# Memory tokens of a two-layer encoder: divided by their root mean square and transposed once, scaled per layer by column; head roots spread by full transposes

## The chip, the cores and the metric

One core of a Trainium2 chip runs the whole program in one launch. The metric is the time of one execution in device microseconds (us). The kernel before ran three times: 1570.52, 1573.77 and 1574.49 us, median 1573.77. One more execution was profiled; it took 1572.0 us, of which 1570.2 us lie between its first and its last recorded instruction (the span).

Engines in the rows: PE is the matrix engine (PEld its weight loads), DVE the vector engine, ACT the scalar engine, POOL the GpSimd, SP the engine that issues nearly all DMAs (SPq is its queue).

## The reference

The reference is an encoder trunk of two layers on x (512 tokens, width 1024), with 256 memory tokens of the same width. What the change touches:

```python
for l in range(2):
    h = rmsnorm(x, g_mix_pre[l])
    ...                                   # h @ w_in[l], split into three head groups
    o_a = diff_attention(...)             # 4 heads, 64 values each
    o_a = rmsnorm(o_a, diff_head_g[l]) * (1.0 - lam_init)     # a norm per head of 64 values
    ...                                   # latent attention o_b, windowed attention o_c
    x = x + rmsnorm(concat([o_a, o_b, o_c]) @ w_out[l], g_mix_post[l])
    xo = cross_attention(rmsnorm(x, g_x_pre[l]), rmsnorm(mem, g_x_mem[l]), w_xq[l], w_xkv[l], w_xo[l])
    x = x + rmsnorm(xo, g_x_post[l])
    ...                                   # SwiGLU feed-forward, added to x in the same way

def rmsnorm(x, g):
    return x * rsqrt(mean(x * x, axis=-1) + 1e-6) * g
```

The memory `mem` is the same in both layers; only its gains `g_x_mem[l]` differ.

## The kernel before

All products take their factors as a high part (type fp32r) and a low part (what the rounding left), and three matmuls stand for one product (`mm3`, lines 149 to 153). A tensor therefore has to be *split*: ACT casts to the high part (L104), DVE subtracts it (L105). Weights come through a ring of two staging tiles `st` (`stage`, L113) and are split into tiles `wh` and `wl`.

A layer begins with `mix_phase`. Attention is cut into units (score, softmax, transposes, values); a loop over t starts one unit per step and runs the later stages of the earlier ones, and beside it draws steps from a generator `fill()`, which holds the products that attention doesn't wait for. How many steps it draws per t follows from the planned PE time of what it has drawn (`FILL_PLAN`, and `FILL_STEP` for each step). Units 0 to 15 are the differential heads (`diff_units`), then come the windowed and the latent ones. The fill is, in this order: the input products of the second pair of differential heads (`in_diff(w, hT, 1, q3b)`), of the windowed keys and values and of half of their queries; then by the string `FILL_ORDER` the steps "q" (other queries), "u" (latent up-projection), "m" (`mem_norm`) and "k" (`make_xK`, keys of the cross-attention); then values and output projection. The scheduler that assigns tiles and order keeps each engine's queue in one fixed order; an engine waits at the head of its queue.

PSUM has two tiles of each of the tags mm, sc, at and av. The tag "at" (name `ps_at`) is where every transpose lands: a transpose waits until one of the two tiles has been read out.

`mem_norm` (L1074 to L1090), in each layer: it loads the gains as a row broadcast over 128 partitions into the slot H3 (L251), loads each half row of the memory into a tile of the tag "o" (L1083), squares it on ACT into what later holds the high part `memTh` (L209) with the sums `rmemss`, forms the root `rmem` on POOL (L213, L214), multiplies by root and gains on DVE (L230), transposes eight blocks of 128x128 on PE (L184), and splits them on ACT and DVE into `memTh` and `memTl`; this for two groups of 128 tokens.

The norm of a differential head, once for each pair of heads (`means`, `rows_`, `norm`): POOL gives `drs`, 8 roots per token (L692); `rows_` turns them into two rows by four thin transposes (L697) and a copy (L698); `norm` spreads the rows over 64 partitions each by a matmul with two ones-rows `halves_r` (L702) and multiplies on DVE (L703).

## Time and profile before

| what | before |
|---|---|
| median of three runs | 1573.77 us |
| the profiled execution | 1572.0 us, span 1570.2 us |
| PE busy | 1545.4 us (98%), 8260 matmul records |
| DVE, ACT, POOL busy | 981.2, 800.4, 96.0 us |
| granted PE clock, mean | 0.995 |
| layer 0: mixing with its fill | about 60 to 300 us |
| layer 1: the same | about 835 to 1080 us |
| DMA | 167.97 MB |

A page of the profile gives the busy time of each engine over the span; a window gives the same for a stretch. Matmuls are pipelined: one of 128 columns is listed with 0.27 us, and the next starts sooner than that. A number in square brackets in a timeline row is how long that engine had been idle before the row, and what ended the idleness. PEclk is the granted clock of PE as a share of 2.4 GHz.

### The profile page before, as it was taken

What the parts mean: (1) busy time and instruction counts of PE and PEld (TensorE: products, weight loads), DVE (VectorE), ACT (ScalarE), POOL (GpSimd) and SP (SyncE); (2) the same over time, 40 slices, a digit from 0 to 9 for tenths busy, and PEclk for the clock granted to TensorE, in tenths of its full rate; (3) what the DMA queues carried; (4) which work ended last, traced back from release to release, by engine and by line L of the source; (5) the groups of instructions that cost most, each with busy time, mean ns of one, the idle gap of its engine ahead of it and who ended that gap; (6) DMA issues with size and microseconds to landing.
All of it is one profiled execution on the core that took longest, in us unless ns stands there. A gap on an engine that the chain in (4) does not pass through costs nothing.

```text
span 1570.2 us, 22003 instructions
## 1 busy us (share of the span) xinstructions
PE 1545.4 (98%) x8260; PEld 1314.0 (84%) x8260; DVE 981.2 (62%) x1933; ACT 800.4 (51%) x1743; POOL 96.0 (6%) x199
## 2 busy tenths in 40 slices
PE   9998999999999999999999999999999999999998
PEld 7887987899888888888888878778888888888886
DVE  7898886764653444455567988857646444444544
ACT  5578888554543222222356788975544532222221
POOL 3100000200200000000130000002002000000000
PEclk9999999999999999999999999999999999999999
DMA  5632651241243232332335234522403423233221
GB/s 164 171 83 88 214 167 46 63 161 54 81 156 112 81 108 81 106 109 81 102 116 145 56 136 163 168 58 90 148 30 104 136 81 107 81 109 106 83 79 54
DMA packets 130195, 167.97 MB, mean 107 GB/s; under 512 B 21796, under 2 KB 100774, under 8 KB 129320
## 3 DMA queue, kind: packets, MB, share of 16 engines
q1 hardware_dynamic: 130080, 166.56, 33.3%
q8 instruction: 65, 1.06, 0.3%
q14 instruction: 42, 0.34, 0.1%
q10 hardware_dynamic: 8, 0.01, 0.0%
HBM read 150.16 MB, written 10.09 MB: 102 GB/s over the span
## 4 chain that ended last, share of the span: by engine, by line
PE 44%; DVE 2%; ACT 2%; POOL 1%; issue 1%; POOLq 0%; DVEq 0%; ACTq 0%
PE ps_mm L153 7%; PE ps_mm L151 7%; PE ps_mm L152 7%; PE ps_av L152 3%; PE ps_av L151 3%; PE ps_av L153 3%; PE ps_sc L151 3%; PE ps_sc L153 3%; PE ps_sc L152 3%; PE ps_at L433 2%; PE ps_av L606 1%; PE ps_sc L818 1%; PE ps_av L607 1%; PE ps_sc L655 1%; ACT hxh L209 0%
## 5 line engine op out<-in xcount | busy, mean ns | idle before, releaser
L105 DVE TENSOR_TENSOR wl<-st,wh 128x512 fp32r<-128x512 f32 (+1 forms) x406 | 273.4, 686 | 249.6 <-ACT wh L104 249.0
L104 ACT CAST wh<-st 128x512 fp32r<-128x512 f32 (+1 forms) x406 | 243.7, 617 | 308.3 <-PE ps_mm L152 126.7
L153 PE MATMUL ps_mm<-hfh,wl 128*128 128x512 f32 (+1 forms) x384 | 142.8, 372 | 2.1 <-DVE wl L105 2.1
L151 PE MATMUL ps_av<-hfh,wh 128*128 128x512 f32 (+1 forms) x384 | 142.9, 372 | 0.0
L152 PE MATMUL ps_mm<-hfl,wh 128*128 128x512 f32 (+1 forms) x384 | 142.6, 371 | 0.0
L151 PE MATMUL ps_mm<-hfh,wh 128*128 128x512 f32 (+1 forms) x384 | 142.6, 371 | 0.0
L153 PE MATMUL ps_av<-hfh,wl 128*128 128x512 f32 (+1 forms) x384 | 142.6, 371 | 0.0
L152 PE MATMUL ps_av<-hfl,wh 128*128 128x512 f32 (+1 forms) x384 | 142.6, 371 | 0.0
L151 PE MATMUL ps_sc<-dwh,f 128*128 128x512 f32 (+1 forms) x322 | 125.1, 389 | 0.5 <-DVE faccSq L1276 0.5
L152 PE MATMUL ps_sc<-dwl,f 128*128 128x512 f32 (+1 forms) x322 | 124.9, 388 | 0.0
L153 PE MATMUL ps_sc<-dwh,f 128*128 128x512 f32 (+1 forms) x322 | 124.9, 388 | 0.0
L104 ACT CAST dwh<-st 128x1024 fp32r<-128x1024 f32 x40 | 40.1, 1050 | 157.0 <-PE ps_sc L153 153.3
L105 DVE TENSOR_TENSOR pl<-ps_at,ph 128x512 fp32r<-128x512 f32 (+1 forms) x128 | 82.6, 654 | 23.9 <-ACT ph L104 22.8
L153 PEld LDWEIGHTS ps_mm<-hfh,wl 128*128 128x128 f32 x384 | 72.3, 188 | 15.1 <-DVE wl L105 2.5
L213 POOL TENSOR_SCALAR rpost<-rpostss 128x1 f32<-128x1 f32 x23 | 11.6, 503 | 1167.8 <-ACT hTh L209 699.2
L151 PEld LDWEIGHTS ps_mm<-hfh,wh 128*128 128x128 f32 x384 | 72.4, 189 | 12.5
L152 PEld LDWEIGHTS ps_av<-hfl,wh 128*128 128x128 f32 x384 | 72.4, 188 | 12.5
L153 PEld LDWEIGHTS ps_av<-hfh,wl 128*128 128x128 f32 x384 | 72.3, 188 | 12.5
L151 PEld LDWEIGHTS ps_av<-hfh,wh 128*128 128x128 f32 x384 | 72.2, 188 | 12.4
L152 PEld LDWEIGHTS ps_mm<-hfl,wh 128*128 128x128 f32 x384 | 72.3, 188 | 12.3
L104 ACT CAST ph<-ps_at 128x512 fp32r<-128x512 f32 (+1 forms) x128 | 70.4, 561 | 23.8 <-PE ps_at L433 22.8
L433 PE MATMUL ps_at<-ident,e 128*128 128x128 f32 x480 | 77.0, 275 | 3.7 <-DVE memTl L105 2.1
(384 smaller groups left out, 3865.3 us busy)
## 6 DMA issues: line engine op xcount, KB each, us to landing
st<-in_w_ffn_in SPq DMA_DIRECT2D x44, 1024.0 KB, 4.9
st<-in_w_ffn_out SPq DMA_DIRECT2D x22, 1024.0 KB, 4.8
st<-in_w_xkv SPq DMA_DIRECT2D x16, 1024.0 KB, 5.4
st<-in_w_in SPq DMA_DIRECT2D x16, 512.0 KB, 4.8
st<-in_w_out SPq DMA_DIRECT2D x16, 512.0 KB, 5.0
st<-in_w_xq SPq DMA_DIRECT2D x8, 1024.0 KB, 5.5
st<-in_w_xo SPq DMA_DIRECT2D x8, 1024.0 KB, 5.0
q<-stg SPq DMA_DIRECT2D x48, 128.0 KB, 2.3
```

What stands on the lines that cost most here:

```text
L104: cast = nc.scalar.copy(hi, src)
L105: nc.vector.tensor_tensor(out=lo, in0=src, in1=hi.bitcast(F32), op=ALU.subtract)
L151: nc.tensor.matmul(ps, lhsT=lh, rhs=rh, start=first, stop=False)
L152: nc.tensor.matmul(ps, lhsT=lh, rhs=rl, start=False, stop=False)
L153: nc.tensor.matmul(ps, lhsT=ll, rhs=rh, start=False, stop=last)
L213: nc.gpsimd.tensor_scalar(out=r, in0=ms[:, 0:1], scalar1=ms[:, 1:2], scalar2=EPS, op0=ALU.add, op1=ALU.add)
L433: nc.tensor.transpose(pt[:, c * P:(c + 1) * P], e[:, k * P:(k + 1) * P], ident)
L606: nc.tensor.matmul(av, lhsT=v, rhs=hi, start=k == u["k0"], stop=False)
L607: nc.tensor.matmul(av, lhsT=v, rhs=lo, start=False, stop=k == u["k1"] - 1)
L655: nc.tensor.matmul(ps, lhsT=t[:, m, 0, i * P:(i + 1) * P], rhs=t[:, m, 1, :], start=True, stop=True)
L818: nc.tensor.matmul(ps, lhsT=mla["qT"][:, h, i * P:(i + 1) * P], rhs=mla["kT"][:, h, :], start=True, stop=True)
```

## The change

It makes three edits. `mem_prep`, new, runs once, as the first four steps of layer 0's fill: it loads the memory, takes the squares (ACT, into the PSUM tile that will hold the transposes), forms the roots (POOL), multiplies by them (ACT), transposes (PE), copies back to the "o" tile (ACT) and stores the result in DRAM as `mem_dram`, laid out with the model's columns on the partitions. In this layout a gain is one number per partition: `gmem` holds the gains of both layers, loaded once. `mem_norm` of each layer then loads `mem_dram` through a staging tile (8 KB per partition) and splits it in eight blocks of 256 tokens, with the gain as the scale of both instructions. The third edit is in the head norm: `spread_` copies each root 64 times along the free dimension on ACT, and four full 128x128 transposes put it on the partitions; the thin transposes, the matmul with `halves_r` and the set-up of `halves_r` go.

```diff
--- before.py
+++ after.py
@@ -277,7 +277,6 @@
     neghalf = cp.tile([P, 8], F32, tag="neghalf", name="neghalf")
     nc.gpsimd.memset(neghalf, -0.5)
     halves_c = cp.tile([P, 2], F32, tag="halves", name="halves")
-    halves_r = cp.tile([2, P], F32, tag="halvesr", name="halvesr")
     nc.gpsimd.memset(halves_c, 0.0)
     for b in range(2):
         nc.gpsimd.memset(halves_c[64 * b:64 * (b + 1), b:b + 1], 1.0)
@@ -297,6 +296,8 @@
     dist_dram = dp.tile([P, NT, S], F32, tag="distd", name="dist_dram")
     dist0 = ap.tile([P, NT, S], F32, tag="dist", name="dist")
     swd_dram = dp.tile([P, 1280], F32, tag="swdd", name="swd_dram")
+    mem_dram = dp.tile([P, KC, MEM], F32, tag="memd", name="mem_dram")
+    gmem = cp.tile([P, DEPTH * KC], F32, tag="gmem", name="gmem")
     cos1 = cp.tile([P, NT, 16], F32, tag="cos1", name="cos1")
     sin2 = mp.tile([P, NT, 32], F32, tag="sin2", name="sin2")
 
@@ -314,9 +315,6 @@
                           diff_lambda.rearrange("l a d -> (l a d)").unsqueeze(0).to_broadcast([P, DEPTH * 128]))
 
     def setup():
-        ph = psum("at")
-        nc.tensor.transpose(ph[0:2, 0:P], halves_c, ident)
-        nc.vector.tensor_copy(out=halves_r, in_=ph[0:2, 0:P])
         nc.vector.tensor_scalar(out=nsinks, in0=sinks, scalar1=-1.0, scalar2=None, op0=ALU.mult)
         lq = tmp("ph", (P, DEPTH * 2, 32))
         lpv = lp.rearrange("p l a b d -> p (l a) b d")
@@ -691,22 +689,21 @@
                                                op0=ALU.mult, op1=ALU.add)
                 nc.gpsimd.tensor_tensor(out=r, in0=r, in1=neghalf, op=ALU.pow)
 
-            def rows_(ch):
-                pt = psum("at")
-                for i in range(NT):
-                    nc.tensor.transpose(pt[0:2, i * P:(i + 1) * P], ch["r"][:, 2 * i:2 * i + 2], ident)
-                nc.scalar.copy(ch["sq"][0:2], pt[0:2])
+            def spread_(ch):
+                nc.scalar.copy(ch["sq"].rearrange("p (n d) -> p n d", d=64),
+                               ch["r"].unsqueeze(2).to_broadcast([P, 8, 64]))
 
             def norm(ch):
                 pr = psum("at")
-                nc.tensor.matmul(pr, lhsT=halves_r, rhs=ch["sq"][0:2], start=True, stop=True)
+                for i in range(NT):
+                    nc.tensor.transpose(pr[:, i * P:(i + 1) * P], ch["sq"][:, i * P:(i + 1) * P], ident)
                 nc.vector.scalar_tensor_tensor(out=ch["o"], in0=ch["o"], scalar=headg, in1=pr,
                                                op0=ALU.mult, op1=ALU.mult)
 
             return chunk_units(
                 score, soft, [[((hh, i), (hh, i + 1), 0, NT) for i in (0, 2)] for hh in range(2)],
                 lambda hh, k: aV[:, k, c, 2 * hh:2 * hh + 2, :].rearrange("p b d -> p (b d)"),
-                [sums_sq, means, nop, rows_, norm, chunk_out(lambda: mdst(c))])
+                [sums_sq, means, nop, spread_, norm, chunk_out(lambda: mdst(c))])
 
         def swa_units(cp_, ip, mdst):
 
@@ -885,7 +882,7 @@
             state["xq"] = [(t[:, 0, k, :], t[:, 1, k, :]) for k in range(KC)], st
 
         def fill():
-            for k, _ in enumerate(seq(in_diff(w, hT, 1, q3b), in_swa_kv(), in_swa_q(0))):
+            for k, _ in enumerate(seq(*([] if l else [mem_prep()]), in_diff(w, hT, 1, q3b), in_swa_kv(), in_swa_q(0))):
                 if k == 0:
                     head.settle()
                 yield
@@ -1071,22 +1068,45 @@
                 as_tile(st_["ps"][i], st_["C"], aT, i * P, 512, (2, 3), first=False)
                 done(i, accs[i], st_["ps"][i])
 
+    def mem_prep():
+
+        with nc.allow_non_contiguous_dma(reason="gains by column, once"):
+            nc.sync.dma_start(gmem, g_x_mem.rearrange("l (k p) -> p (l k)", p=P))
+        for t in range(2):
+            hs = []
+            ms = small(2, "rmemss")
+            for j in range(2):
+                m = tmp("o")
+                nc.sync.dma_start(m, mem[0, t * P:(t + 1) * P, 512 * j:512 * (j + 1)])
+                pt = psum("at")
+                nc.scalar.activation(pt, m, AF.Square, scale=1.0 / 32.0, accum_out=ms[:, j:j + 1])
+                hs.append((m, pt))
+            r = small(1, "rmem")
+            nc.gpsimd.tensor_scalar(out=r, in0=ms[:, 0:1], scalar1=ms[:, 1:2], scalar2=EPS, op0=ALU.add, op1=ALU.add)
+            nc.gpsimd.tensor_tensor(out=r, in0=r, in1=neghalf[:, :1], op=ALU.pow)
+            yield
+            for j, (m, pt) in enumerate(hs):
+                nc.scalar.activation(m, m, AF.Copy, scale=r)
+                for c in range(4):
+                    nc.tensor.transpose(pt[:, c * P:(c + 1) * P], m[:, c * P:(c + 1) * P], ident)
+                nc.scalar.copy(m, pt)
+                nc.sync.dma_start(mem_dram[:, 4 * j:4 * j + 4, t * P:(t + 1) * P], m.rearrange("p (c t) -> p c t", t=P))
+            yield
+
     def mem_norm(l):
         memT = Split8(("H2", "dist"), MEM, "memT")
 
         def gen():
-            g, = gains("H3", g_x_mem[l])
-            for t in range(2):
-                hs = []
-                for j in range(2):
-                    m = tmp("o")
-                    nc.sync.dma_start(m, mem[0, t * P:(t + 1) * P, 512 * j:512 * (j + 1)])
-                    hs.append(m)
-                parts = norm_to_T(hs, g, memT, t * P, "rmem", hs)
-                yield
-                for f in parts:
-                    f()
-                yield
+            st = stage((), KC, MEM)
+            nc.sync.dma_start(st, mem_dram)
+            for k in range(KC):
+                g = gmem[:, KC * l + k:KC * l + k + 1]
+                hi = memT.h(k)
+                nc.scalar.activation(hi, st[:, k, :], AF.Copy, scale=g)
+                nc.vector.scalar_tensor_tensor(out=memT.l(k), in0=st[:, k, :], scalar=g, in1=hi.bitcast(F32),
+                                               op0=ALU.mult, op1=ALU.subtract)
+                if k % 2:
+                    yield
         return memT, gen()
 
     def make_xK(l, memT):
```

How the instructions move, on two engines and one queue. First PE in layer 0, in the key half of the input product of the second differential pair (products L151 to L153 into `ps_mm`; L655, in the changed kernel L653, are scores; L433 are the transposes of the attention weights `e`). Before:

```order
L153 MATMUL ps_mm<-hTh_146,wl 128x512
L151 MATMUL ps_mm<-hTh_146,wh 128x512
L152 MATMUL ps_mm<-hTl_147,wh 128x512
L153 MATMUL ps_mm<-hTh_146,wl 128x512
L433 MATMUL ps_at<-ident,e 128x128 x4
L655 MATMUL ps_sc<-q_00_561 128x512 x2
L433 MATMUL ps_at<-ident,e 128x128 x4
```

And in the changed kernel (L1091 are the transposes of the memory, L941 one of a latent tile):

```order
L151 MATMUL ps_mm<-hTh_147,wh 128x512
L1091 MATMUL ps_at<-ident,o 128x128 x4
L152 MATMUL ps_mm<-hTl_148,wh 128x512
L1091 MATMUL ps_at<-ident,o 128x128 x4
L153 MATMUL ps_mm<-hTh_147,wl 128x512
L151 MATMUL ps_mm<-hTh_147,wh 128x512
L152 MATMUL ps_mm<-hTl_148,wh 128x512
L941 MATMUL ps_at<-ident,m 128x128
```

The first eight memory transposes stand sixteen products into this half; the first transposes of `e` come only after the second eight, one input product later, where the queue reads:

```order
L153 MATMUL ps_mm<-hTh_147,wl 128x512
L1091 MATMUL ps_at<-ident,o 128x128 x4
L152 MATMUL ps_mm<-hTl_146,wh 128x512
L1091 MATMUL ps_at<-ident,o 128x128 x4
L153 MATMUL ps_mm<-hTh_145,wl 128x512
L151 MATMUL ps_mm<-hTh_145,wh 128x512
L431 MATMUL ps_at<-ident,e 128x128 x8
```

Next the SP queue of layer 0 about that place. Before (L372 stores a table that POOL has built, L495 to L497 bring the second differential pair's queries and keys into place, L113 loads weights):

```order
L351 DMA dist_dram<-dist 128x2048
L113 DMA st<-in_w_in 128x8x256
L372 DMA swd_dram<-swd 128x1280
L113 DMA st<-in_w_in 128x8x64 x3
L495 DMA q_10_1040<-stg 32x2x512
L496 DMA q_10_1040<-stg 32x2x512
L497 DMA q_10_1040<-stg 32x1024
```

In the changed kernel:

```order
L349 DMA dist_dram<-dist 128x2048
L1080 DMA o<-in_mem 128x512 x2
L370 DMA swd_dram<-swd 128x1280
L113 DMA st<-in_w_in 128x8x256
L113 DMA st<-in_w_in 128x8x64
L1093 DMA mem_dram<-o 128x4x128 x2
L493 DMA q_10_1091<-stg 32x2x512
L1080 DMA o<-in_mem 128x512 x2
L494 DMA q_10_1091<-stg 32x2x512
```

The second two loads of the memory stand behind the first of the `q` transfers, and the weights of the windowed keys behind the store of the table.

Last PE in layer 1, where the memory's transposes of this layer stood. Before:

```order
L607 MATMUL ps_av<-pl,aV 128x256
L184 MATMUL ps_at<-ident,o 128x128 x8
L433 MATMUL ps_at<-ident,e 128x128 x4
L606 MATMUL ps_av<-ph,KScV 128x256
L800 MATMUL ps_at<-ident,m 96x128 x8
```

In the changed kernel:

```order
L605 MATMUL ps_av<-pl,aV 128x256
L431 MATMUL ps_at<-ident,e 128x128 x4
L797 MATMUL ps_at<-ident,m 96x128 x8
L151 MATMUL ps_mm<-wh,latT 128x384
L152 MATMUL ps_mm<-wl,latT 128x384
```

The eight transposes are gone from between the values of one unit (L607) and the transposes of the next (L433), and so are the eight that followed later in this layer.

## Rows read from the trace of the kernel before

**Rows 1.** The page's first part: busy time, share of the span, instructions.
```profile
PE 1545.4 (98%) x8260; PEld 1314.0 (84%) x8260; DVE 981.2 (62%) x1933; ACT 800.4 (51%) x1743; POOL 96.0 (6%) x199
```
**Rows 2.** Windows of layer 0: stretch, length, busy by engine, PEclk, DMA share, GB/s.
```profile
60.00:90.00 30.00, 30.00 (x150) 24.75 (x149) 27.00 (x72) 23.23 (x54) 4.34 (x12) 1.00 0.47 110
90.00:125.00 35.00, 34.88 (x188) 29.11 (x187) 33.43 (x83) 27.49 (x61) 1.65 (x1) 1.00 0.24 65
132.00:142.00 10.00, 6.02 (x39) 4.69 (x38) 7.80 (x22) 8.88 (x21) 0.00 (x0) 1.00 0.46 151
142.00:145.60 3.60, 3.60 (x18) 3.32 (x17) 3.11 (x12) 3.14 (x11) 0.86 (x2) 0.53 0.00 0
```
**Rows 3.** Windows of layer 1.
```profile
900.00:912.00 12.00, 11.98 (x72) 9.81 (x71) 11.05 (x31) 11.44 (x30) 1.80 (x3) 1.00 0.65 218
912.00:917.00 5.00, 2.73 (x19) 1.87 (x18) 4.68 (x11) 4.95 (x12) 0.00 (x0) 1.00 0.32 107
917.00:920.50 3.50, 3.50 (x17) 3.41 (x16) 2.94 (x11) 3.19 (x10) 0.86 (x2) 0.51 0.00 0
```
**Rows 4.** Timeline of PE, layer 0: start, us, line, operation, [idle before, who ended it].
```profile
137.71 1.35 PE L184 MATMUL ps_at<-ident,o 128*128 128x128 f32 x8 [0.59 <-DVE sr L742]
140.21 0.66 PE L433 MATMUL ps_at<-ident,e 128*128 128x128 f32 x4 [1.15 <-DVE memTl L105]
141.59 0.38 PE L606 MATMUL ps_av<-ph,KScV 128*128 128x256 f32 x1 [0.73 <-ACT ph L104]
```
**Rows 5.** Timeline of PE, layer 1, the same place.
```profile
913.07 1.35 PE L184 MATMUL ps_at<-ident,o 128*128 128x128 f32 x8 [0.53 <-DVE sr L742]
915.34 0.66 PE L433 MATMUL ps_at<-ident,e 128*128 128x128 f32 x4 [0.92 <-DVE memTl L105]
```
**Rows 6.** Timeline of ACT, layer 0: a weight cast that waits for its load.
```profile
133.04 0.62 ACT L104 CAST wh<-st 128x512 fp32r<-128x512 f32 x1 [1.62 <-DMA st<-in_w_xkv]
```
**Rows 7.** Timeline of PE, layer 0: the head norm's thin transposes and its matmul.
```profile
125.80 0.60 PE L697 MATMUL ps_at<-ident,drs 128*2 128x128 f32 x4
...
129.32 1.12 PE L702 MATMUL ps_at<-c,halvesr 2*128 2x512 f32 x2
```
**Rows 8.** Groups by line and shape: busy us, mean ns, idle before.
```profile
L209 ACT ACTIVATE memTh<-o 128x512 fp32r<-128x512 f32 x8 | 5.0, 627 | 0.0
L209 ACT ACTIVATION_READ_ACCUMULATOR memTh<-o 128x1 f32 x8 | 1.5, 191 | 0.0
L104 ACT CAST ph<-ps_at 128x512 fp32r<-128x512 f32 x112 | 64.9, 587 | 23.7 <-PE ps_at L433 22.8
L587 ACT ACTIVATE e<-e,mr 128x512 f32<-128x512 f32 x32 | 21.8, 734 | 0.1
L587 ACT ACTIVATE e<-e,sr 128x256 f32<-128x256 f32 x16 | 8.2, 513 | 1.7 <-DVE sr L742 1.7
L230 DVE SCALAR_TENSOR_TENSOR o<-o,rmem,gains 128x512 f32<-128x512 f32 x8 | 5.9, 743 | 1.0 <-POOL rmem L214 1.0
L105 DVE TENSOR_TENSOR memTl<-ps_at,memTh 128x512 fp32r<-128x512 f32 x8 | 5.5, 686 | 1.7 <-ACT memTh L104 1.7
```
**Rows 9.** One tile, `rmem`, on POOL: count, ns min/median/max, first and last start.
```profile
L213 POOL TENSOR_SCALAR rmem<-rmemss x4: 299/299/301, 127.4 to 918.2; 128x1 f32<-128x1 f32 x4
L214 POOL TENSOR_TENSOR rmem<-rmem,neghalf x4: 557/560/569, 127.7 to 918.6; 128x1 f32<-128x1 f32 x4
```
**Rows 10.** Timeline of ACT, layer 0, early: an exponential, the first casts of `ph`.
```profile
66.96 0.72 ACT L669 ACTIVATE e<-e,dnm 128x512 f32<-128x512 f32 x1 [0.23 <-DVE dnm L659]
...
73.42 1.07 ACT L104 CAST ph<-ps_at 128x512 fp32r<-128x512 f32 x2
```
**Rows 11.** Timeline of PE, layer 0, early: the first transposes of attention weights.
```profile
72.36 0.60 PE L433 MATMUL ps_at<-ident,e 128*128 128x128 f32 x4
```
**Rows 12.** Timeline of SP's queue: the first transfer of `q`.
```profile
73.54 0.62 SPq L495 DMA_DIRECT2D q<-stg  x1
```
**Rows 13.** DMA issues: form, KB each, median us from issue to landing.
```profile
o<-in_mem SPq DMA_DIRECT2D x8, 256.0 KB, 2.9
```

## The prediction

> **What bounds the kernel now.** I read the page's first part, then windows over both mixing phases, then PE's timeline where it has gaps. The reader is to see that PE is busy for 98% of the span [rows 1], so that work taken from PE counts wherever PE is not waiting, and that the little waiting it does is not spread evenly. From 60 to 125 us PE has no gap to speak of (30.00 of 30.00 and 34.88 of 35.00 us), while DVE is busy for 27.00 and 33.43 us [rows 2]: two full engines, neither with room for delay. From 132 to 142 us PE is busy for 6.02 of 10 us, and in the 3.6 us after it the granted clock is 0.53 of 2.4 GHz, which is mostly the 1.2 GHz level [rows 2]. Layer 1 repeats it: 2.73 of 5.00 us from 912 on, then 0.51 for 3.5 us [rows 3]. Both gaps lie at the memory's transposes: PE waits 0.59 us before them (the queue names a neighbour on DVE, which stands between the two multiplications by root and gains), then 1.15 us until DVE has read out their PSUM tile, then 0.73 us for the attention weights that were queued behind [rows 4]; layer 1 shows the first two again [rows 5]. In layer 0 a part of the gap has another origin: ACT stands 1.62 us before a weight cast until `w_xkv` lands [rows 6], and the casts of `ph` that PE needs are behind it.
>
> **The change part by part.** All against the profiled execution, 1572.0 us (span 1570.2 us and 1.8 us around it); the median of the three runs is 1.8 us above that execution.
>
> Head norm, four times in the kernel. Gone are four thin transposes and one matmul in two passes, added are four full transposes. A thin transpose already streams 128 columns: four are busy for 0.60 us [rows 7], and four full ones for the same 0.60 us [rows 11]; with 0.27 us for one they start 0.11 us apart, and the exchange of four for four costs nothing. The matmul's two passes take 1.12 us [rows 7]; four times that is 4.5 us. The copy on ACT stays a copy of 512 elements; its broadcast reading is not in the trace, and I take it between a cast of 512 (0.587 us) and a scaling of 512 (0.734 us) [rows 8], a difference of 0.6 us over four that nobody sees. PE has 11.98 of 12.00 us in the stretch where one of these matmuls stands [rows 3], so I count it nearly whole: **4.2 us less**; if ACT sets the pace there (11.44 of 12.00 us [rows 3]) it is nothing.
>
> The memory in layer 1. Sixteen transposes go: 16 x 0.11 = 1.8 us of PE. The idle time from 912 to 917 us is 5.00 - 2.73 = 2.3 us [rows 3]. Not all of it comes back, since ACT is busy for 4.95 of these 5.00 us. What ACT does for the memory falls from four squares (0.627 + 0.191 us) and four casts out of PSUM (0.587 us), 5.6 us, to eight scalings of 256 columns; the nearest row is 0.513 us [rows 8], so 4.1 us. That relief of 1.5 us, and the transposes no longer holding `ps_at`, I take as half of the idle time, 1.15 us. On DVE four multiplications (0.743 us) and four subtractions (0.686 us), 5.7 us, become eight scaled subtractions of half the size; between no gain and half, and I count none, since DVE's queue is not what PE waits for once the transposes are gone. With the gap shortened, the clock should not fall: 3.5 us at 0.51 lose 1.7 us. Sum 1.8 + 1.15 + 1.7 = **4.65 us less**, with bounds 0 (ACT sets the end) and 1.8 + 2.3 + 1.7 = 5.8 us.
>
> The memory in layer 0, late part. The same 1.8 us of transposes leave this place, the idle time is 10.00 - 6.02 = 4.0 us, of which I take half, 2.0 us, and the clock 3.6 x 0.47 = 1.7 us. The broadcast gains, half a megabyte, no longer travel beside `w_xkv`; in their place a full megabyte `mem_dram` is loaded through the staging ring, ahead of the weights. So the wait of rows 6 may go or may only move. **5.5 us less**, bounds 0 and 7.5 us.
>
> The memory in layer 0, new early part. Here the change pays. The sixteen transposes arrive in a stretch without gaps, 1.8 us. ACT gets four squares (0.82 us with their read-out), four scalings (0.734 us), four copies from PSUM (0.587 us), together 8.5 us, in 60 to 90 us, where it has 30.00 - 23.23 = 6.8 us free [rows 2]; this is no loss by itself. The chain is: squares, root, scaling, transposes, copies, and PE's fixed order stands in the middle of it. First half: the squares follow the exponential of 66.96 us [rows 10], end 1.64 us after its 0.9 us, at 69.5; the root takes 0.30 + 0.56 us [rows 9], 70.4; the two scalings end at 71.1 and 71.8. PE reaches the first transposes eight products, 0.2 us each (150 in 30 us [rows 2]), before the 72.36 us at which this input product ended [rows 11], at 70.7. It waits 0.4 us, then 0.7 until the second scaling: 1.1 us. Second half: its loads stand behind the first transfer of `q`, which starts at 73.54 us [rows 12] and now some 2 us later; 0.6 us of issue, 2.9 us of flight [rows 13], squares 1.64, root 0.86 and scaling 0.73 make 82.3 us. PE comes there one input product later (24 products, scores and transposes, some 30 matmuls at 0.2 us, 6 us after 73 us, plus the 2 us), about 81: it waits 1.3 us, and then, at the transposes of `e` behind, 1.0 us for ACT's copies out of both `ps_at` tiles. These transposes of `e` were read out at 73.42 us [rows 10] and now at about 83 us. Attention goes on meanwhile, since there are five tiles `e`, but units are held up at the fifth; DVE has only 3 us free in 60 to 90 us and 1.6 us in the next 35 [rows 2], so what it loses it keeps lost. I put that at 1.4 us. Together 1.8 + 1.1 + 1.3 + 1.0 + 1.4 = **6.6 us more**; bounds 1.8 us (everything but the columns is hidden) and 1.8 + 9.7 = 11.5 us (the whole lateness of the `ph` casts, 83.1 - 73.4, lost).
>
> The store of the halves (four of 256 KB) and the load of the gains by column, 2048 elements of 4 bytes, run at a time when nobody waits for these queues; I cost them at nothing. If that cover is gone, the loads behind them are late by a flight of about 3 us [rows 13]. The set-up's transposition and copy are 0.3 us, at nothing.
>
> Sum: -4.2 - 4.65 - 5.5 + 6.6 = -7.75 us, 1564.25 us for the profiled execution, and with the 1.8 us by which the median lies above it, **1566 us**.
>
> Beside the transposes' rows: the Trainium skill, "TensorE: Matmul & The Clock Gate", section "Part 4: PE-mode transpose", puts one transpose at about 275 ns in a kernel's context. The trace agrees on the duration, 0.27 us, but not on what it costs in a row of four, 0.11 us; by the page's figure the sixteen would be 4.4 us, layer 1 would gain 2.6 us more and layer 0 would neither gain nor lose, 1563 us.
>
> **The rivals.**
>
> *Everything comes back.* The waits early are hidden behind products that the trace of before doesn't show beside them, and both late gaps close. For it: the gaps have the memory's transposes on both sides [rows 4, 5]. Against: ACT at 4.95 of 5.00 us. -4.5 - 5.8 - 7.5 + 1.8 = -16 us: 1558 us.
>
> *The early part eats it.* The `ph` casts' lateness is passed on whole, since from 60 to 125 us PE and DVE are both full. -4.2 - 4.65 - 5.5 + 11.5 = -2.85 us: 1571 us. For it: rows 2; against: five tiles of `e`, and the scores of the next units run on.
>
> *Slower: the early waits cost the clock, too, and the late gaps stay.* PE waits between 70 and 85 us the way it did ahead of the two falls, the granted clock goes to the 1.2 GHz level there too, in a stretch with no slack, and the late gaps remain because ACT sets them. For it: each of the two falls follows a stretch with waits around eight such transposes [rows 2, 3], and each of the two early pairs is just that. Against: my waits there, 2.3 us at most, have products between them. It is slower than before as soon as the early part costs more than the 6.0 us that stay, the norm's 4.2 and layer 1's columns 1.8. Price: early 11.5 + 1.7 for the clock, less 6.0: +7.2 us, 1581 us.
>
> **How the numbers follow.** The forecast, 46%; everything comes back, 16%; the early part eats it, 28%; slower, 10%. A change within 0.3% (4.7 us) can't be told from none. The first two are faster by more than that, though the forecast's edge touches it, and I leave 61% for faster; the third is the same, 29%; the last slower, 10%. The range must hold 8 in 10: from 1557 us, just under the second case, to 1577 us, above the third and short of the last. The forecast's own range is 1560 to 1570 us.
>
> **What would show it.** In the changed profile: no matmul in the head norm; no gap at about 910 us, and PEclk 1.00 in the windows there and at about 142 us; between 68 and 85 us a wait of PE at each of the two pairs of memory transposes on ACT's scaling, the second larger, and the first casts of `ph` after 80 us. Wrong would be a wait of over 3 us at one of these, a fall of the clock before 100 us, a weight cast in 130 to 160 us that waits for its load longer than 1.6 us, or a mixing phase of layer 1 that ends no earlier, relative to its start, although the transposes are gone.

## The result, and the profile after

The changed kernel takes 1583.26 us (median of four runs, 1581.78 to 1585.97); the kernel before, run beside it, 1573.85 us. The ratio is 1.0066, 95% interval 1.0054 to 1.0079: some 10 us slower, where 1566 us were forecast. Its profiled execution has a span of 1582.0 us, 11.8 us more than that of before.

The first part of its page answers to [rows 1]: PE has 4.8 us more busy time, although the norm took work from it.

```profile
PE 1550.2 (98%) x8235; PEld 1317.8 (83%) x8235; DVE 977.3 (62%) x1932; ACT 803.5 (51%) x1751; POOL 93.8 (6%) x195
```

Windows of the changed kernel, columns as in [rows 2]; the first two stretches are those of [rows 2], the others are where the granted clock fell and what lies ahead of it in layer 1.

```profile
60.00:90.00 30.00, 27.52 (x134) 21.10 (x134) 19.06 (x50) 22.23 (x52) 6.10 (x16) 1.00 0.52 148
90.00:125.00 35.00, 33.55 (x167) 25.84 (x165) 33.98 (x85) 30.24 (x68) 0.00 (x0) 0.94 0.41 85
120.50:127.50 7.00, 6.91 (x26) 5.66 (x25) 6.94 (x19) 4.17 (x10) 0.00 (x0) 0.51 0.00 0
154.50:158.20 3.70, 3.70 (x18) 3.38 (x18) 2.63 (x11) 2.70 (x7) 0.00 (x0) 0.54 0.79 247
246.80:250.30 3.50, 3.50 (x15) 2.87 (x13) 2.08 (x5) 2.88 (x8) 0.00 (x0) 0.51 0.01 2
922.00:926.00 4.00, 2.63 (x18) 1.98 (x17) 3.90 (x14) 4.00 (x12) 0.00 (x0) 1.00 0.00 2
926.00:933.00 7.00, 6.32 (x26) 5.77 (x26) 5.69 (x21) 6.11 (x17) 0.00 (x0) 0.51 0.00 0
```

The number that matters is DVE's in the first row: 19.06 us of 30, where it had 27.00 [rows 2]. DVE then is full (33.98 of 35) and can't make it up. Nobody had put work on DVE or taken any from it here: it was starved. The rest of the chain, in the changed kernel, ACT's timeline first:

```profile
79.96 0.60 ACT L1082 ACTIVATE ps_at<-o 128x512 f32<-128x512 f32 x1 [1.58 <-DMA o<-in_mem]
81.24 0.60 ACT L1082 ACTIVATE ps_at<-o 128x512 f32<-128x512 f32 x1 [0.56 <-DMA o<-in_mem]
83.05 1.33 ACT L1089 ACTIVATE o<-o,rmem 128x512 f32<-128x512 f32 x2 [0.38 <-POOL rmem L1086]
84.76 1.07 ACT L1092 COPY o<-ps_at 128x512 f32<-128x512 f32 x2
86.46 1.07 ACT L104 CAST ph<-ps_at 128x512 fp32r<-128x512 f32 x2
```

SP's queue, from the store of the first half to the load of the second:

```profile
72.58 0.92 SPq L1093 DMA_DIRECT2D mem_dram<-o  x2
74.54 0.61 SPq L493 DMA_DIRECT2D q<-stg  x1
76.45 1.08 SPq L1080 DMA_DIRECT2D o<-in_mem  x2
```

PE's timeline, and DVE's longest wait:

```profile
74.91 0.50 PE L653 MATMUL ps_sc<-q 96*128 96x512 f32 x1 [0.56 <-DVE dnm L657]
77.19 0.50 PE L151 MATMUL ps_mm<-hTh,wh 128*128 128x512 f32 x1 [1.02 <-ACT wh L104]
83.83 0.66 PE L1091 MATMUL ps_at<-ident,o 128*128 128x128 f32 x4 [0.63 <-ACT o L1089]
85.45 1.09 PE L431 MATMUL ps_at<-ident,e 128*128 128x128 f32 x8
```

```profile
86.47 0.68 DVE L545 TENSOR_TENSOR KScV<-ps_mm,KScV 64x512 fp32r<-64x512 f32 x1 [5.51 <-ACT KScV L544]
```

The second half can be loaded only when the first has been stored (both live in the two tiles `o`), so its squares wait until 80 us (SP's queue stands 1.2 us for the store to land, and the load then takes over 3 us); the transposes of `e`, behind them in PE's order, start at 85.45 us instead of 72.36 [rows 11], and the first casts of `ph` at 86.46 instead of 73.42 [rows 10].

How late each stage is against the kernel before, in us, from the start of the same product in both traces (the last score of the differential units, and the first and the last L151 product with `memTh` as its first factor, in layer 0; layer 0's last L153 product with `mixT` into `ps_mm`; then layer 1's last score of the differential units, its last L151 product with `memTh` as its first factor, its last latent score, and the last product of all). Some profiled executions begin their first input product into `ps_mm` 3.0 to 3.2 us later; that is subtracted.

| kernel | scores | `memTh` first | last | layer 0 | scores | `memTh` last | latent | end |
|---|---|---|---|---|---|---|---|---|
| before, at us | 122.0 | 149.4 | 188.7 | 284.3 | 899.1 | 963.8 | 1041.7 | 1563.3 |
| changed | +10.2 | +8.3 | +6.4 | +11.1 | +11.1 | +9.9 | +11.7 | +11.8 |
| memory only | +8.4 | +5.2 | +5.1 | +9.9 | +9.8 | +5.5 | +6.3 | +6.3 |
| tiles `c` | +6.7 | +4.0 | +2.4 | +4.9 | +4.8 | +1.7 | +1.9 | +1.9 |
| loads in the set-up | +6.9 | +3.1 | +1.9 | +1.9 | +2.1 | +0.5 | +0.3 | +0.5 |
| without transposes | +7.5 | +11.9 | +10.9 | +13.3 | +13.3 | +12.8 | +12.3 | +12.3 |
| norm only, ACT | -0.1 | +1.4 | -0.6 | -0.4 | -0.4 | -0.8 | +0.3 | +0.4 |
| norm only, POOL | -0.1 | +0.2 | -2.6 | -2.6 | -2.5 | -4.0 | -3.0 | -2.9 |
| layer 1 only, spread | 0.0 | -0.6 | -0.5 | -0.5 | +1.3 | -3.0 | -0.6 | -0.4 |

The row of the changed kernel reads: 10 us lost by 122 us, nearly 4 won back where the memory's transposes used to stand, nearly 5 lost again at the end of layer 0's mixing; in layer 1 only 1.2 won and 1.8 lost.

### The profile page after: what moved, and what is told of

Its sections match the earlier page's. It is cut to its first block, busy times and chain, and to the rows that moved or that the text cites. A ratio compares the mean times of both kernels' runs of the same rounds, so it can differ in the third digit from the quotient of the medians.

```text
span 1582.0 us, 21953 instructions
## 1 busy us (share of the span) xinstructions
PE 1550.2 (98%) x8235; PEld 1317.8 (83%) x8235; DVE 977.3 (62%) x1932; ACT 803.5 (51%) x1751; POOL 93.8 (6%) x195
## 5 line engine op out<-in xcount | busy, mean ns | idle before, releaser
L153 PE MATMUL ps_mm<-hfh,wl 128*128 128x512 f32 (+1 forms) x384 | 142.8, 372 | 2.0 <-DVE wl L105 2.0
L151 PE MATMUL ps_av<-hfh,wh 128*128 128x512 f32 (+1 forms) x384 | 142.9, 372 | 0.0
L153 PE MATMUL ps_av<-hfh,wl 128*128 128x512 f32 (+1 forms) x384 | 142.6, 371 | 0.0
L151 PE MATMUL ps_mm<-hfh,wh 128*128 128x512 f32 (+1 forms) x384 | 142.6, 371 | 0.0
L151 PE MATMUL ps_sc<-dwh,f 128*128 128x512 f32 (+1 forms) x322 | 125.2, 389 | 0.5 <-DVE faccSq L1296 0.5
L153 PE MATMUL ps_sc<-dwh,f 128*128 128x512 f32 (+1 forms) x322 | 124.9, 388 | 0.0
L153 PEld LDWEIGHTS ps_mm<-hfh,wl 128*128 128x128 f32 x384 | 72.3, 188 | 14.9 <-DVE wl L105 2.5
L151 PEld LDWEIGHTS ps_mm<-hfh,wh 128*128 128x128 f32 x384 | 72.4, 188 | 12.4
L153 PEld LDWEIGHTS ps_av<-hfh,wl 128*128 128x128 f32 x384 | 72.3, 188 | 12.4
L151 PEld LDWEIGHTS ps_av<-hfh,wh 128*128 128x128 f32 x384 | 72.3, 188 | 12.3
L213 POOL TENSOR_SCALAR rpost<-rpostss 128x1 f32<-128x1 f32 x23 | 11.1, 485 | 1171.4 <-ACT hTh L209 699.1
```

The costliest lines, as they stand in the source:

```text
L151: nc.tensor.matmul(ps, lhsT=lh, rhs=rh, start=first, stop=False)
L153: nc.tensor.matmul(ps, lhsT=ll, rhs=rh, start=False, stop=last)
L213: nc.gpsimd.tensor_scalar(out=r, in0=ms[:, 0:1], scalar1=ms[:, 1:2], scalar2=EPS, op0=ALU.add, op1=ALU.add)
```

## The experiments

Times are medians; a ratio is to the kernel before on the same chip, with its interval.

**Which edit.** Three kernels: before with the norm's edit; the changed kernel with the old norm; before with the preparation in layer 0's feed-forward and only layer 1 split from `mem_dram` (of this one, the lines in the feed-forward):

```diff
             fs.append(gate_up(g))
+            if l == 0 and g == 4:
+                run_all(mem_prep())
```

> The kernel before with the head norm's edit alone (spread copy, four full transposes in place of thin transposes, copy and two-pass matmul). Theory A (the norm is worth what its matmul took from PE, and the loss of the changed kernel lies in the memory edit): 4.2 us less than before, 3 to 4.5. Rival B (ACT sets the pace where the norm stands, so PE's columns are worth little): 0 to 1.5 us less. If the time rises, both are wrong and the loss sits in the norm.

> The changed kernel with the old head norm (two constant tiles of scales joined into one to make room; otherwise only the memory edit). Theory A: some 14 us more than before (the changed kernel's 10 and the norm's 4.2). Rival B: 10 to 11.5 us more. The two edits together should give the changed kernel's difference if they don't interact.

> The kernel before, with layer 0's memory untouched, the once-only preparation put into layer 0's feed-forward (after its fifth group, where ACT and DVE are half idle) and layer 1's memory split from the stored tile. It leaves the early cost out. The prediction's late gain: layer 1 gives 4.65 us, the sixteen transposes in the feed-forward cost 1.8: 2.85 us less than before. Theory C (in layer 1 the scalings on ACT stand in the same place as the squares and casts did, and the gaps and the clock fall stay): the trace of the changed kernel moves 1.2 us towards before in layer 1's first half with 2.1 us of the norm in it, and 1.8 us away later; so the memory edit alone gives 0.9 + 1.8 more in layer 1 and 1.8 in the feed-forward, 4.5 us more than before.

Measured: norm only 1574.47 us, 1.0000 (0.9989 to 1.0011); memory only 1579.83 us, 1.0036 (1.0022 to 1.0050); layer 1 only 1575.55 us, 1.0011 (0.9999 to 1.0023). The norm's edit is worth nothing and not 4.2 us, and on top of the memory it costs 4.7 us more (1.0066 against 1.0036, the intervals just apart). Layer 1 gained 4.0 us and gave 2.2 back, so neither the forecast (-2.85) nor theory C (+4.5) held; the feed-forward became 3.9 us longer, because PE came to the transposes before the scaling was done:

```profile
582.89 0.66 PE L1096 MATMUL ps_at<-ident,o 128*128 128x128 f32 x4 [1.88 <-ACT o L1094]
```

**The early loss.** Kernels that change only how the preparation is placed. Tiles `c` for the second half; the preparation behind the input products; loads in the set-up into `ph` and `pl`; PSUM `av` in place of `at`; `av` and `c` together (one line of each edit, the longest shortened; the comments name the kernel):

```diff
-                m = tmp("o")
+                m = tmp("oc"[t])               # tiles c
+                m = tmp(("ph", "pl")[j])       # set-up, drawn ahead of the loop
-                pt = psum("at")
+                pt = psum("av")                # av
-seq(mem_prep(), in_diff(w, hT, 1, q3b), in_swa_kv(), in_swa_q(0))
+seq(in_diff(w, hT, 1, q3b), in_swa_kv(), in_swa_q(0), mem_prep())   # behind
```

> The changed kernel with the second half of the memory loaded into the tiles c and not o, so that its load doesn't wait until the first half is stored; nothing else changed in the program, though the fixed order of PE changes with it: the first transposes of e then stand 18 matmuls later than in the kernel before, not 48. Theory D (the early loss is that the transposes of e, fixed behind the second pair of memory transposes, start at 85 us and not at 72): they start at about 77 us, and of the 11 us by which layer 0 ends late some 6 come back: 1577 us. Rival E (the late scalings on ACT and the load through the staging ring make the loss): no change from 1583 us, within 2.

> The changed kernel with the memory's preparation drawn after the input products of the fill and not ahead of them; nothing else changed. The first transposes of e stand where they stood in the kernel before. Theory D (the early loss comes from the transposes of e that stood behind the memory's): DVE is busy again for over 18 of 20 us in 70 to 90 us, the units are no later than before at 122 us, and of the 11.7 us that the changed kernel is late there, what comes back is that without the two memory waits at their new place: 1574 to 1577 us. Rival E (the cost is that of the preparation itself, its work on ACT and PE beside full engines): the lateness only moves to 110 to 140 us, 1581 to 1584 us.

> The changed kernel with the memory loaded during the set-up into four tiles of their own (those of ph and pl, which attention uses later), so that neither load waits for a store; the preparation is drawn ahead of the attention loop. PE has the sixteen transposes eight products apart and the first transposes of e right behind, 16 matmuls later than in the kernel before. Theory D: the first ph casts at about 74 to 76 us, DVE over 18 of 20 us busy in 70 to 90 us, the early lateness 2 to 4 us in place of 11.7: 1574 to 1577 us. Rival E (cost of the preparation's own work): no more than the tiles c gave, 1578 us or above.

> The changed kernel with the memory's squares and transposes in the PSUM tiles av and not at; loads, store and ring of the tiles o as in the changed kernel. PE's fixed order then has the memory's transposes at the same products as the changed kernel, but the first transposes of e ahead of the second pair, 7 matmuls later than in the kernel before (48 in the changed kernel). Theory D (the loss came from the transposes of e that stood behind the second pair, which waited for a load behind a store): the first casts of ph at 74 to 76 us, DVE busy for over 16 us of 70 to 90 (19.5 before, 11.4 in the changed kernel), 4 to 7 us less than the changed kernel's 1583. Rival E (whatever order, the preparation's own work costs it): 1581 us or above.

> The changed kernel with both: the second half of the memory in the tiles c, and squares and transposes in the PSUM tiles av. Theory D (the early loss is the two rings, o and at): 7 to 9 us less than the changed kernel, 1574.5 to 1576.5 us, no lateness of the units above 3 us at 122 us. Rival E (a part is the work on ACT, PE and DVE beside full engines, and neither ring gives it back): no better than the tiles c alone, 1578 to 1579 us, with the units some 6 us late at 122 us.

Measured: tiles `c` 1578.65 us, 1.0030 (1.0018 to 1.0042); behind the input products 1579.75 us, 1.0045 (1.0027 to 1.0062), the lateness only moved, 11.4 us at 122 us in the trace; set-up 1576.36 us, 1.0011 (0.9998 to 1.0023); `av` 1580.32 us, 1.0041 (1.0027 to 1.0055); both 1580.96 us, 1.0044 (1.0026 to 1.0063). Theory D holds for half: without the wait for the store 5.7 us came back; the set-up's time lies in D's range, but its units are 6.9 us late at 122 us and not 2 to 4; and with `av` the `ph` casts came in time but the next one did not. In the kernel with `av`, on ACT:

```profile
75.66 1.08 ACT L104 CAST ph<-ps_at 128x512 fp32r<-128x512 f32 x2
86.74 0.59 ACT L104 CAST ph<-ps_at 128x512 fp32r<-128x512 f32 x1 [0.40 <-PE ps_av L604]
```

With both rings out of the way the differential units were still 7.3 us late. What was left to blame was the work itself, so the last kernel takes before and adds the preparation (loads, squares, roots, scalings, copies, stores; tiles `o` and `c`, PSUM `av`) without its transposes:

```diff
                 nc.scalar.activation(m, m, AF.Copy, scale=r)
-                for c in range(4):
-                    nc.tensor.transpose(pt[:, c * P:(c + 1) * P], m[:, c * P:(c + 1) * P], ident)
                 nc.scalar.copy(m, pt)
```

> The kernel before, with the preparation's loads, squares, root, scalings, copies and stores as the first four steps of layer 0's fill (tiles o and c, PSUM av), but without its sixteen transposes; what it stores is not used. Theory E (the rest of the early lateness is the preparation's work on ACT and what stands behind it): the units 4 to 7 us late at 122 us, 3 to 6 us more than before. Rival J (it is the transposes, at which PE waits in its fixed order): the units at most 2 us late, within 1.5 us of before.

Measured: 1588.02 us, 1.0084 (1.0067 to 1.0101). The units are 7.5 us late at 122 us, with not one transpose added, so theory E holds. Part of the 7.5 may be the clock's: this execution spends 6.8 us from 81.4 us on at the 1.2 GHz level, up to 3.4 us; the 4.1 that are left are still in E's range and above J's 2. That of all this work it is ACT's part which counts is read from ACT's timeline (everything in this execution is 3.2 us later than in before):

```profile
73.32 1.34 ACT L1091 ACTIVATE o<-o,rmem 128x512 f32<-128x512 f32 x2 [0.38 <-POOL rmem L1088]
74.57 1.05 ACT L1092 COPY o<-ps_av 128x512 f32<-128x512 f32 x2
...
77.93 1.34 ACT L1091 ACTIVATE c<-c,rmem 128x512 f32<-128x512 f32 x2 [0.61 <-POOL rmem L1088]
79.17 1.05 ACT L1092 COPY c<-ps_av 128x512 f32<-128x512 f32 x2
80.11 0.59 ACT L104 CAST ph<-ps_at 128x512 fp32r<-128x512 f32 x1
```

PE did its first transposes of `e` when it always does (75.61 us, less 3.2), but their cast stood in ACT's queue behind this block until 80.11 us, and DVE waited 1.48 us for it. Here 4.4 us more were lost by the first product with `memTh`, since layer 0's old `mem_norm` then follows; that this comes from it is argued, not tried.

**The norm.** The matmul of before issued twice; then the copy on POOL, in before with the norm's edit alone, in the changed kernel, and in two of the kernels above:

```diff
+                nc.tensor.matmul(pr, lhsT=halves_r, rhs=ch["sq"][0:2], start=True, stop=True)   # twice
-                nc.scalar.copy(ch["sq"].rearrange("p (n d) -> p n d", d=64),
+                nc.gpsimd.tensor_copy(out=ch["sq"].rearrange("p (n d) -> p n d", d=64), in_=...
```

> The kernel before with the norm's two-pass matmul issued twice, four times 1.12 us more on PE and nothing else; the output is the same. Theory F (where the norm stands, PE waits for ACT and DVE anyway, so that what the new norm took from PE became waiting): under 1 us more. Rival G (PE's columns count there, and the norm's edit gave nothing because its broadcast copy on ACT cost as much): 4 to 4.5 us more.

> The kernel with the norm's edit alone, the spread copy on POOL and not on ACT. With the copy on ACT the norm's edit gave 0.0 us. Theory F (where the norm stands, ACT is the engine that is full, so PE's 4.5 us became waiting): taking 0.6 us four times from ACT brings 1.5 to 4 us, 1570 to 1573 us. Rival I (what PE gave up is waited out for other reasons, DVE and the order of units): no change, within 1 us of before.

> The changed kernel with the norm's spread copy on POOL and not on ACT. Theory F (the copy on ACT is what the norm's edit costs, in the changed kernel as alone): 4 to 5 us less than the changed kernel's 1583. Rival (in the changed kernel DVE is what is full where the norm stands, after the early loss): no change, 1582 to 1584 us.

> The same with the norm's copy on POOL as well. If the copy on ACT costs 4.4 us wherever the rest is: 4 to 5 us less than the kernel with both rings undone.

> The changed kernel with the memory loaded in the set-up into four tiles of their own (1.7 us above before) and the norm's copy on POOL. If the copy is worth here what it was in three other kernels (4.4 to 4.7 us): 2.7 us less than before, 1571 to 1573 us. If the late part gives it back: 1574 to 1576 us.

Measured: matmul twice 1578.55 us, 1.0026 (1.0014 to 1.0039), nearer to G: PE's columns do count there, though the trace has only 2.3 of the 4.1 us. Norm with POOL 1568.95 us, 0.9972 (0.9961 to 0.9982), the lowest median of all: 4.4 us less, and 4.2 had been forecast. Changed kernel with POOL 1579.64 us, 1.0036 (1.0021 to 1.0051), against 1.0066; `av` and `c` with POOL 1577.91 us, 1.0016 (1.0004 to 1.0029), against 1.0044; set-up with POOL 1573.43 us, 0.9993 (0.9978 to 1.0008), against 1.0011. So the copy's place is worth 3 to 5 us in each of four pairs; in the first two the intervals are apart, in the other two they overlap. With both repairs (set-up and POOL) the change comes out even with before. ACT's row for the copy in the kernel with the norm alone, and what its view of line 691 says:

```profile
127.13 0.62 ACT L691 COPY c<-drs 128x512 f32<-128x512 f32 x1 [1.60 <-POOL drs L688]
127.77 0.59 ACT L104 CAST ph<-ps_at 128x512 fp32r<-128x512 f32 x1
```

```profile
L691 ACT COPY c<-drs x4: 617/618/619, 127.1 to 937.6; 128x512 f32<-128x512 f32 x4
  POOL drs L688: 6.0, 3
```

The copy itself lasts what it was estimated to, 0.618 us. But it reads POOL's root directly, and POOL takes 1.65 us for that: ACT stood 6.0 us in all, with a `ph` cast behind. In before ACT had a copy there too, of 0.576 us, but it came after four transposes, and no wait stood ahead of it: ACT's work is the same within 0.2 us over four, and the wait is what is new. In the changed kernel:

```profile
130.70 0.62 ACT L693 COPY c<-drs 128x512 f32<-128x512 f32 x1 [2.71 <-POOL drs L690]
912.10 0.62 ACT L693 COPY c<-drs 128x512 f32<-128x512 f32 x1 [1.59 <-POOL drs L690]
```

On POOL it follows the root at once and lasts no longer (median of four 0.622 us):

```profile
122.19 1.65 POOL L688 TENSOR_TENSOR drs<-drs,neghalf 128x8 f32<-128x8 f32 x1 [54.53 <-DVE drs L686]
123.91 0.62 POOL L691 COPY c<-drs 128x512 f32<-128x512 f32 x1
```

The Trainium skill ("GPSIMD Engine Reference", section "4.1 Engine selection") puts an elementwise operation with one input at about the line rate on this engine; the trace agrees for this copy, 0.62 us on both, but not for the scaling further down, which takes 0.928 us where ACT takes 0.506.

**Layer 1.** The preparation drawn in four steps, in the feed-forward's groups 3 to 6; with the new norm (copy on ACT); with layer 1's scalings on POOL; with the norm on POOL:

```diff
-            if l == 0 and g == 4:
-                run_all(mem_prep())
+            if l == 0 and 3 <= g < 7:
+                ...
+                next(state["prep"])
-                nc.scalar.activation(hi, st[:, k, :], AF.Copy, scale=g)
+                nc.gpsimd.tensor_scalar(out=hi, in0=st[:, k, :], scalar1=g, scalar2=None, op0=ALU.mult)   # e12 alone
```

> The kernel with layer 1 alone from the stored memory, its preparation in layer 0's feed-forward now drawn in four steps over four groups, so that PE doesn't come to the transposes before the scaling is done. With the preparation in one step the feed-forward became 3.9 us longer, of which 1.8 are the transposes' columns, and layer 1 gained 4.0 us and gave 2.2 back. Theory H (the rest of the 3.9 is waiting for loads and scalings): the feed-forward 1.8 to 2.2 us longer, 1573 to 1574.5 us, up to 1 us below before. Rival: the waits stay, 1575 to 1576 us.

> Layer 1 from the stored memory with the preparation spread over four groups of layer 0's feed-forward, and the new norm in both layers. Apart they measured 1.7 us less than before and 0.0. If they don't interact: 1.7 less. If layer 1's shorter fill leaves PE waiting for ACT, so that the norm's ACT copy counts: no gain or slower than before. If the norm's columns come to count once the memory's transposes are gone: 3 to 4 us less.

> Layer 1 from the stored memory as in the run with four steps, with the eight scalings of layer 1 on POOL and not on ACT. Theory C (in layer 1 ACT's scalings hold up exponentials and casts, and that is why the gaps there stay and the clock falls): 3.6 us of ACT work go, the gain in layer 1 grows by 1 to 3 us, 1570 to 1572.5 us. Rival (the end of the mixing phase is set by the attention units, and what the fill gains earlier is given back there): the fill's products over the memory start earlier, but the phase ends at the same time, 1573 us.

> The norm with its copy on POOL, and layer 1 from the stored memory with the preparation in four steps in layer 0's feed-forward; layer 0's memory as before. If the two add: 4.4 + 1.7 = 6.1 us less than before, 1568 us. If layer 1's gain is given back at the end of its mixing phase whatever shortens the fill: no better than the norm alone, 4.4 less.

Measured: four steps 1573.11 us, 0.9989 (0.9976 to 1.0002): the feed-forward is 1.8 us longer, which is 16 x 0.11, and theory H holds. With the norm 1574.10 us, 1.0006 (0.9995 to 1.0017): 2.7 us more than without it, though the intervals overlap; the copy on ACT seems to cost here too. Scalings on POOL 1575.28 us, 1.0009 (1.0000 to 1.0018): no gain, against theory C; it looks worse than the four steps on ACT, but the intervals just overlap. POOL needs 0.928 us for one of 256 columns, ACT 0.506. Both faster edits together 1572.45 us, 0.9984 (0.9973 to 0.9996): they don't add (the sum of both would be 0.9961), and nothing shows them better than the norm with POOL alone (0.9961 to 0.9982).

Where layer 1's gain is given back, ACT has one more wait, at the cast of the cross-attention's query weights `w_xq`. In before:

```profile
236.35 0.64 ACT L104 CAST q<-st 128x512 fp32r<-128x512 f32 x1
1011.66 0.62 ACT L104 CAST q<-st 128x512 fp32r<-128x512 f32 x1 [0.90 <-DMA st<-in_w_xq]
```

In the changed kernel, and behind the first one PE's wait for a `ph` cast that stood in ACT's queue after it:

```profile
243.79 0.62 ACT L104 CAST q<-st 128x512 fp32r<-128x512 f32 x1 [2.46 <-DMA st<-in_w_xq]
1022.31 0.62 ACT L104 CAST q<-st 128x512 fp32r<-128x512 f32 x1 [1.77 <-DMA st<-in_w_xq]
```

```profile
245.67 0.38 PE L604 MATMUL ps_av<-ph,mV 128*128 128x256 f32 x1 [1.92 <-ACT ph L104]
```

And in layer 1 with four steps:

```profile
1013.11 0.62 ACT L104 CAST q<-st 128x512 fp32r<-128x512 f32 x1 [2.10 <-DMA st<-in_w_xq]
```

In the set-up kernel, which gave nothing back, this cast did not wait in layer 0 and 0.70 us in layer 1. The load was not moved in an experiment, so the link is read from traces; in layer 0 they line up well. Between the columns `memTh` last and layer 0 of the table, kernels whose cast did not wait lost 0.2 us at most (set-up, both with the norm only, layer 1 only), those with a wait of 1.20 and 1.24 us lost 2.4 to 2.5 (tiles `c`, without transposes), those with 2.46 and 2.53 us lost 4.7 and 4.8 (changed, memory only; these two also have a fall of the clock there, 3.4 us at the 1.2 GHz level). In layer 1 the order is looser: 1.75 us of wait went with 0.8 lost (memory only), 1.77 with 1.8.

## Why the prediction was wrong, point by point

By the changed kernel's row of the table, the 19.5 us between the sum (-7.75) and the trace (+11.8) are: 3.6 us more for the early part, 1.7 less won in layer 0's late part, 4.7 lost behind it that the sum had no term for, 3.4 less won in layer 1, 1.8 lost behind that, again without a term, and the norm's 4.2, which no stage shows.

**The early part was mis-sized.** The forecast gave it 6.6 us; the trace has 10.2 at the last differential score. Of the waits it named, the one at the first pair hardly came (0.15 us, against 1.1), the one at the second was 0.63 us, against 1.3, and the first `ph` casts came at 86.46, against 83. Two steps failed. "This is no loss by itself" of 8.5 us of ACT in a stretch with 6.8 us free: the experiment without transposes shows 7.5 us of lateness, at least 4.1 with its fall of the clock taken off, and in its trace the casts that feed DVE stand behind that work in one queue. And "attention goes on meanwhile", with 1.4 us for DVE: DVE lost 8 us of 30, while the casts came 13.0 us late; the rival "the early part eats it", with 11.5 us for this part, was nearer. The load of the second half was placed right in the queue, but its wait of 1.2 us for the store was not in the working; that it was issued at 76.45 us, near the 76.1 of the working, is luck, since `q` ahead of it came 1 us sooner than taken.

**The norm's 4.2 us were right for PE and lost on ACT.** The failed step is that the copy on ACT is a difference "that nobody sees". Its length was right; what was missed is the wait that the edit adds, for POOL's root, ahead of ACT's queue. With the copy on POOL the edit gives 4.4 us, close to the 4.2, though in part by luck: that move also takes the copy of 0.6 us off ACT four times, which the sum did not have. The transposes cost what the sum took, 0.11 us each: the feed-forward became 1.8 us longer with sixteen of them. The 275 ns of the Trainium skill ("TensorE: Matmul & The Clock Gate", section "Part 4: PE-mode transpose") would have made it 4.4, by an estimate of sixteen times that; the measurement decides for the row.

**The late terms were of the right kind, and not kept.** Forecast 5.5 us in layer 0 and 4.65 in layer 1. With the memory edit alone the lateness falls from 8.4 us at the last differential score to 5.1 at the last `memTh` product (by 4.3 with tiles `c`, by 5.0 with the set-up), and in layer 1 from 9.8 to 5.5. What was to be named is what is late next: the load of `w_xq`, which ACT meets at the head of its queue, as the prediction feared for the wait of [rows 6] (it "may only move"; in the changed kernel no weight cast waits for its load between 130 and 165 us). One of the prediction's signs of being wrong came, too: layer 1's mixing ended no earlier, +11.7 after +11.1. In the changed kernel layer 1 kept 1.2 us, and PE waited for ACT, now behind the scalings. PE there:

```profile
923.64 0.38 PE L604 MATMUL ps_av<-ph,aV 128*128 128x256 f32 x1 [0.44 <-ACT ph L104]
925.80 0.86 PE L431 MATMUL ps_at<-ident,e 128*128 128x128 f32 x4 [0.82 <-ACT e L585]
928.20 1.09 PE L797 MATMUL ps_at<-ident,m 128*96 128x128 f32 x4 [0.68 <-ACT qT L798]
```

On ACT, there:

```profile
924.44 0.91 ACT L1105 ACTIVATE memTh<-st,gmem 128x256 fp32r<-128x256 f32 x2
925.24 0.51 ACT L585 ACTIVATE e<-e,sr 128x256 f32<-128x256 f32 x1
925.64 0.91 ACT L1105 ACTIVATE memTh<-st,gmem 128x256 fp32r<-128x256 f32 x2
```

This looks like the bound "ACT sets the end", for which the profile had 4.95 of 5.00 us [rows 3]. But the kernels with tiles `c` and with the preparation behind run the same program in layer 1, PE's order the same row for row, and won 3.0 us there; neither has a fall of the clock in that stretch, where the changed kernel's execution has 6.8 us at the 1.2 GHz level. The memory edit without the copy on ACT won 4.3 us (memory only, layer 1 only with four steps), close to the 4.65. So that bound was not reached; what separates 1.2 from 3.0 us in one and the same program, the fall or the waits ahead of it, is open.

**The clock.** It was to stay up at 142 and 912 us. It did not fall there, but at 120.6, 154.7, 246.9, 926.1 and 1025.1 us, 23.9 us at the 1.2 GHz level against 6.8 in before (one fall at 8 to 9 us and one behind the last product, which both have, not counted): up to 8.5 us of the 11.8 in this execution. Most of the loss does not need them: the changed kernel's three other runs had a mean granted clock of 0.994 to 0.996, where the profiled one had 0.990 and before's 0.995, and took 1581.78 to 1585.97 us. And the fall at 120.6 us cost little: from the last but two to the last but one differential score the lateness rises by 4.4 us across it, and by 3.8 in the memory edit alone, which has no fall there. The rival "slower" ended at 1581 us, near the measured time, by luck: it has a fall in 70 to 85 us that this execution doesn't have, and still counts the norm's 4.2 us as won. The memory edit alone has such a fall at 77.4 us, the kernel with `av` at 80.5.

**Open.** How much of a single execution is the clock's and how much the waits'; why the cast of `w_xq` waits for its load in layer 0 with tiles `c` and not with the set-up, which is most of what the set-up won more; whether the copy on ACT would cost nothing one step later, when the root is done, which was not tried; and what the matmul issued twice cost beyond the trace's 2.3 us.

## What to carry to other kernels

An edit that takes work from the busiest engine can be paid by the engine that hands it its operands: list every instruction that is put on that engine's queue, what it waits for, and which hand-over stands behind it, even where the engine is idle for a quarter of the stretch. Where a second engine is nearly full, count each microsecond that its feed comes late as lost. And ask of an early gain which load the faster engine will meet next.

## What the runs showed of the hardware

Profiled executions begin in two ways, though the kernels have the same work there. In before PE has 44 matmuls from 6 to 15 us:

```profile
6.00:15.00 9.00, 9.00 (x44) 5.90 (x43) 6.81 (x11) 7.08 (x17) 2.75 (x6) 0.81 1.06 371
```

In the profiled execution of the kernel with tiles `c` it has 24, and everything after is 3.2 us later:

```profile
6.00:15.00 9.00, 9.00 (x24) 4.35 (x23) 4.52 (x7) 4.24 (x9) 1.10 (x3) 1.00 1.06 354
```

The second row's PEclk of 1.00 is no reading: the trace's first entry of the clock is at 14.1 us in that execution, at 5.6 us in before. The matmuls tell it. The same four start at 5.25 us in both, first before, then tiles `c`:

```profile
5.25 2.15 PE L1331 MATMUL ps_mm<-e,c 1*128 1x512 f32 x4
```

```profile
5.25 3.78 PE L1351 MATMUL ps_mm<-e,c 1*128 1x512 f32 x4
```

So PE ran slower for longer at the start there; by the first L151 product (12.15 and 14.75 us) 2.6 of the 3.2 us are lost.

The clock's falls differ as well where the order doesn't: in layer 1 PE's queue is the same, row for row, in the changed kernel, with tiles `c` and with the preparation behind, and the profiled executions had 10.2, 0 and 3.4 us at the 1.2 GHz level there, and became 0.6 us later, 2.9 and 1.3 us earlier.
